# A hybrid encoder step on one Trainium2 core: three plain column tiles, x staged once in two tiles, the first weight pair prepared beside them, operands of the second half built in fixed slots

## The chip, the core and the metric

The kernel runs on one core of a Trainium2 chip. A core has TensorE (PE, matrix products; PEld is its weight load), VectorE (DVE), ScalarE (ACT), GpSimd (POOL) and SyncE (SP, which here issues nearly all DMAs). Each engine works through its own queue in order, and semaphores tie the queues together. The metric is the device time of one execution in microseconds (us).

## The reference, cut to what matters

Two layers on 1024 prompt tokens and 64 sample tokens (1088 columns in all), model width 1024, fp32. Only the first layer, a gated short convolution, is touched by the change:

```
h = rms_norm(x, g)                                  # 1088 x 1024
b, c, xv, z = split(h @ w_in, 4)                    # w_in: 1024 x 4096
u = c * xv
conv = u[t-2]*cw[0] + u[t-1]*cw[1] + u[t]*cw[2]     # causal, per channel
y = (silu(z) * b * conv) @ w_out
x = x + y
```

The second layer is multi-head latent attention over the prompt in chunks of 64 and over a cache of 512 positions for the sample, with a SiLU gate and an output product; a final RMSNorm ends the step. Outputs are both y, the last two convolution rows, and the latents and rope keys.

## The kernel before, in words

Everything is kept transposed: 128 channels on the partitions, tokens on the free axis. To reach fp32 precision each operand is split into a high part in TensorE's reduced fp32 format (a copy on ScalarE) and a low part, the difference (a subtraction on GpSimd or VectorE); a product is then three matmuls: high x high, high x low, low x high.

The input product is worked through in column tiles `ct` of 128 output channels (8 of them) and two token halves of 544 columns (`sc` 0 and 1; `SC` = 544), each half in two chunks of 272 (`NS`).

- **Plain tiles.** For `ct` 0 and 1 the first half is done directly (lines 776 to 834): for each of the four weight parts (order `PARTS`), and for each chunk `c`, `conv_mm` makes 24 matmuls of 272 columns into one PSUM bank, and `conv_evac` takes it out on VectorE. The banks go round in turn (`gps`, line 236), eight of them in this stage. Bank 7 is also where `conv_tail` (line 467) sums the convolution. In tile 0 the order of work on ScalarE, VectorE, GpSimd and TensorE is that of the program text (`keep_order`, `pe_order`); later the Tile framework orders each engine's queue by its own cost model.
- **x.** `x_dma` loads x of the first half in chunks of 272 columns into eight slots of the tile `STG`; chunk 1 goes into the slots of chunk 0. `build_dma` loads the first half a second time, in pieces of 544 columns and four at a time, and then the second half twice: once for the sum of squares (`load_half`, line 592) and once for the operands.
- **Pairs.** All other tiles are done by a seven-product scheme (Strassen's, in Winograd's form) over pairs of weight parts: `u` from parts 1 and 2, `z` from parts 3 and 0. A pair has the seven products p1 to p7, each 4 x 3 matmuls of 272 columns, and PSUM banks 0 to 4 as accumulators; the last two products of a pair (p3, p4) are run inside the next pair. `build(sc, k)` (line 543) makes the token-side operands of the scheme (seven combinations of the four blocks of x, split high and low) for `k` = 0 to 3 into `R2` (first half) or `R1` (second half). `prep` (line 637) makes the weight side: it loads the two parts, splits them as they are (`unit`, 1024 wide, the low part on GpSimd, into three rotating buffer pairs `whi`/`wlo` twice and `bhi`/`blo` once), and makes three sums of 512 columns with PSUM banks 5 and 6 (`S1`, `S2`) and the SBUF tile `t4`; the low parts of the first two are made on VectorE, that of the third (`t4l`) on GpSimd (line 667).
- **Around them.** `run` (line 700) goes through 12 pairs of the first half (`ct` 2 to 7) and 16 of the second, and after each product does one step of `prep` for the next pair and one step of the job list (`side`). The job list holds first the builds of the first half (in tile 1), then `second_half`: loads and squares of the second half, its norm factors, and its builds, which run on GpSimd and ScalarE, with the scaling on ScalarE and VectorE through PSUM. `whole` (line 859) makes pair 12, the first of the second half, wait until the job list is empty.
- **After a product.** `put` in `conv_pairs` (line 743) takes out each of the four blocks of a pair: blocks 11 and 22 are added into the tile `u` or `z`; 12 and 21 are multiplied onto it. For `z` the SiLU of part 3 is applied on ScalarE to blocks 11 and 21 (lines 746 and 751). Block 21 is product p4, in the bank that p1 of the next pair but one takes over.

The rest of the kernel (output product of the convolution, layer 2, final norm) follows behind and is the same text after the change.

Of the kernel before, what the change touches and what calls it, by code (L numbers as in the profile page):

```python
# [19 lines left out]
D = 1024  # L20
# [189 lines left out]
def kernel(ctx, tc, xT, small, w1, w2, w3, w3r, wpair, wqr, wv, wkT, w4,  # L210
# [61 lines left out]
    hi_on = [None]  # L272

    def load_w(src, n, view=None, into=None, lo_engine=None, cuts=None, shared=False):
# [17 lines left out]
        ordered((lo_engine or G).tensor_sub(lo[:, :m], raw[:, :m], r32(hi[:, :m])))  # L292
# [111 lines left out]
    YLB = p1.tile([P, 2, T], F32R, name="YLB")  # L404
# [4 lines left out]
    def yl(k, c0, c1):  # L409
        return YLV[:, k, c0:c1] if k < 6 else YLB[:, k - 6, c0:c1]  # L410

# [6 lines left out]

    def x_dma(c, k):
        XS[k] = STG[:, k * NS:(k + 1) * NS]  # L420
        SP.dma_start(out=XS[k], in_=xT[k][:, c * NS:(c + 1) * NS])
# [116 lines left out]
    def build_dma(sc, k):  # L538
        for i in range(2):
            o = (2 * (k % 2) + i) * SC  # L540
            SP.dma_start(out=STG[:, o:o + SC], in_=xT[k + 4 * i][:, sc * SC:(sc + 1) * SC])

    def build(sc, k):
        h, l = [x[:, :, k] for x in SETS[sc]]
        a, b = [STG[:, (2 * (k % 2) + i) * SC:(2 * (k % 2) + i + 1) * SC] for i in range(2)]
        halves = lambda x: x.rearrange("p (s n) -> p s n", s=2)
# [22 lines left out]
        yield  # L569
        put(1, b)  # L570
# [6 lines left out]
        put(3, a)  # L577
        yield
        put(5, b)
        yield  # L580

    jobs = []

    def side(n=1):

        while n and jobs:
            if next(jobs[0], 0) == 0:
                jobs.pop(0)
            else:
                n -= 1  # L590

    def load_half():

        slot = lambda k: STG[:, (k % 4) * SC:(k % 4 + 1) * SC]
        for k in range(KD):
            if k < 3:
                SP.dma_start(out=slot(k), in_=xT[k][:, SC:])
        yield
        yield
        for k in range(KD):  # L600
            if k + 3 < KD:
                SP.dma_start(out=slot(k + 3), in_=xT[k + 3][:, SC:])
            if k == 0:
                A.activation(out=rb[:, SC:], in_=slot(k), func=AF.Square)
            else:
                A.activation(out=slot(k), in_=slot(k), func=AF.Square)
                G.tensor_add(rb[:, SC:], rb[:, SC:], slot(k))
            yield
# [63 lines left out]
    def product(f, name):  # L672
# [27 lines left out]
    def run(pairs):  # L700

        steps = {}
        for n, f in enumerate(pairs):
            f.set = n % 2
# [1199 lines left out]
```

## Time and profile before

| | |
|---|---|
| time, median of 3 runs | 1140.75 us (1140.28 to 1142.57) |
| profiled execution | 1142.36 us, span 1140.6 us |
| mean granted TensorE clock | 0.971 of full speed |
| PE busy | 1060.4 us (93%), 7099 matmuls |
| PEld busy | 1010.8 us (89%) |
| DVE busy | 769.5 us (67%) |
| ACT busy | 645.8 us (57%) |
| POOL busy | 541.7 us (47%) |
| DMA | 119.02 MB, mean 104 GB/s |
| chain that ended last | PE 58%, DVE 8%, issue 6%, POOL 5%, DMA 4%, ACT 4% |

The page also cuts the span into 40 slices of 28.5 us. In tenths, PE's busy share and its granted clock (9 is 90% or more) are:

```profile
PE   8778997998999999999998999999999999999994
PEclk8897999999999999999998999999999999999997
```

The slices below 9 in the first third lie in the convolution layer, which ends at 427.8 us. Busy times of different engines overlap, and matmuls are pipelined, so that a busy PE is not necessarily at its peak rate; where PE's time goes is read from the count of matmuls in a stage and the time of one.

### The profile page before, as it was taken

Reading aid. Unit: us, or ns where it says so; the run is one execution under the profiler, and the core shown is the slowest. Engines: PE = TensorE matmul, PEld = TensorE weight load, DVE = VectorE, ACT = ScalarE, POOL = GpSimd, SP = SyncE. Lnnn points to the kernel's source line nnn. Section 1 sums busy time; section 2 is a strip of 40 time slices with the busy share of each in tenths; the row PEclk is TensorE's granted clock in tenths of the full one; section 3 lists DMA queues with packets and bytes.
Section 4 is the critical chain, followed back from the end, with each engine's and each line's share of the span. In section 5 each row is a group of like instructions: output and inputs, shape, how many; then the busy total and the mean of one; then the engine's idle time right before and its main releaser. Section 6 shows DMA issues by size and latency. Waiting matters only on the chain.

```text
span 1140.6 us, 19740 instructions
## 1 busy us (share of the span) xinstructions
PE 1060.4 (93%) x7099; PEld 1010.8 (89%) x7099; DVE 769.5 (67%) x1530; ACT 645.8 (57%) x1402; POOL 541.7 (47%) x454
## 2 busy tenths in 40 slices
PE   8778997998999999999998999999999999999994
PEld 7777887898999999999888999899998999988983
DVE  6597665656666655555799533488888888886466
ACT  6246566565656653334542334677877788786452
POOL 3246488777656552112335223254644555464243
PEclk8897999999999999999998999999999999999997
DMA  7226333434232323432313211542243412335224
GB/s 220 88 82 202 103 104 118 128 109 130 81 112 77 109 97 128 147 126 86 100 61 129 76 51 47 144 105 65 61 96 84 101 47 56 75 116 181 89 92 150
DMA packets 60450, 119.02 MB, mean 104 GB/s; under 512 B 8336, under 2 KB 32656, under 8 KB 60352
## 3 DMA queue, kind: packets, MB, share of 16 engines
q1 hardware_dynamic: 60144, 117.43, 34.3%
q8 instruction: 56, 0.92, 0.3%
q14 instruction: 42, 0.34, 0.1%
q10 hardware_dynamic: 144, 0.26, 0.1%
q0 software_dynamic: 64, 0.07, 0.0%
HBM read 83.72 MB, written 16.31 MB: 88 GB/s over the span
## 4 chain that ended last, share of the span: by engine, by line
PE 58%; DVE 8%; issue 6%; POOL 5%; DMA 4%; ACT 4%; SPq 1%; POOLq 0%; ACTq 0%; DVEq 0%
PE PS L299 39%; PE PS L1430 15%; PE PS L1469 4%; DMA QB<-stg 3%; POOL wlo L1708 1%; POOL t4l L622 1%; POOL wlo L622 1%; ACT PH L1482 1%; ACT stg L1546 1%; DVE OL L954 1%; DVE t L666 1%; SPq L1556 1%; DVE PL L1486 0%; DVE qt L1155 0%; DVE SZ L365 0%
## 5 line engine op out<-in xcount | busy, mean ns | idle before, releaser
L299 PE MATMUL PS<-R,whi 128*128 128x272 f32 (+2 forms) x1598 | 368.7, 315 | 30.5 <-DVE z L753 7.7
L299 PEld LDWEIGHTS PS<-R,whi 128*128 128x128 f32 x1598 | 272.0, 192 | 37.6 <-DVE z L753 9.0
L299 PE MATMUL PS<-R,wlo 128*128 128x272 f32 (+2 forms) x856 | 267.5, 314 | 4.8 <-POOL wlo L622 3.6
L299 PEld LDWEIGHTS PS<-R,wlo 128*128 128x128 f32 x856 | 163.6, 192 | 5.7 <-POOL wlo L622 3.8
L292 POOL TENSOR_TENSOR wlo<-wraw,whi 128x1024 fp32r<-128x1024 f32 x32 | 78.8, 2463 | 184.7 <-ACT whi L288 178.8
L1430 PE MATMUL PS<-KB,QB 96*128 96x512 f32 (+11 forms) x576 | 125.4, 355 | 1.3 <-DMA QB<-stg 0.6
L1430 PEld LDWEIGHTS PS<-KB,QB 96*128 96x128 f32 (+1 forms) x576 | 94.4, 190 | 9.9 <-DVE PL L1486 1.1
L1447 DVE TENSOR_REDUCE st<-PS 128x1 f32<-128x1024 f32 (+7 forms) x128 | 94.7, 749 | 11.2 <-PE PS L1430 10.4
L1464 POOL TENSOR_SCALAR Pt<-Pt,st 128x640 f32<-128x640 f32 (+3 forms) x64 | 61.6, 965 | 85.3 <-DVE st L1460 84.7
L1486 DVE TENSOR_TENSOR PL<-PS,PH 128x512 fp32r<-128x512 f32 (+3 forms) x192 | 98.8, 548 | 3.1 <-ACT PH L1482 1.8
L1482 ACT CAST PH<-PS 128x512 fp32r<-128x512 f32 (+3 forms) x192 | 85.4, 496 | 15.4 <-PE PS L1469 14.1
L622 POOL TENSOR_TENSOR wlo<-wraw,whi 128x1024 fp32r<-128x1024 f32 x28 | 67.6, 2414 | 49.5 <-ACT whi L621 49.5
L1430 PE MATMUL PS<-PH,VB 128*128 128x256 f32 x320 | 76.5, 278 | 0.0
L1430 PE MATMUL PS<-PL,VB 128*128 128x256 f32 x320 | 75.2, 281 | 0.2 <-DVE PL L1486 0.2
L299 PE MATMUL PS<-R,bhi 128*128 128x272 f32 x320 | 62.1, 292 | 5.0 <-DVE z L753 2.4
L1456 ACT ACTIVATE Pt<-PS,st 128x640 f32<-128x640 f32 (+3 forms) x64 | 62.1, 970 | 5.7 <-DVE st L1460 2.6
L1430 PEld LDWEIGHTS PS<-PH,VB 128*128 128x128 f32 x320 | 60.7, 190 | 1.4 <-DVE PL L1486 0.8
L1430 PEld LDWEIGHTS PS<-PL,VB 128*128 128x128 f32 x320 | 61.0, 190 | 0.7 <-DVE PL L1486 0.4
L288 ACT CAST whi<-wraw 128x1024 fp32r<-128x1024 f32 (+1 forms) x33 | 34.1, 1032 | 46.2 <-PE PS L299 23.2
L299 PEld LDWEIGHTS PS<-R,bhi 128*128 128x128 f32 x320 | 50.3, 191 | 6.3 <-DVE z L753 3.3
L1469 PE MATMUL PS<-ident,Pt 128*128 128x128 f32 x416 | 55.4, 273 | 0.2 <-ACT Pt L1456 0.2
L1464 POOL TENSOR_SCALAR Ph<-Ph,st 128x512 f32<-128x512 f32 (+3 forms) x64 | 34.2, 535 | 39.0 <-DVE st L1460 28.6
(414 smaller groups left out, 2721.7 us busy)
## 6 DMA issues: line engine op xcount, KB each, us to landing
wraw<-in_w SPq DMA_DIRECT2D x82, 512.0 KB, 3.6
KB<-stg SPq DMA_DIRECT2D x32, 256.0 KB, 3.8
QB<-stg SPq DMA_DIRECT2D x32, 256.0 KB, 4.3
braw<-in_w SPq DMA_DIRECT2D x14, 512.0 KB, 4.6
STG<-in_xT SPq DMA_DIRECT2D x24, 272.0 KB, 3.1
QB<-qr_scratch SPq DMA_DIRECT2D x32, 128.0 KB, 2.9
x<-x_scratch SPq DMA_DIRECT2D x8, 416.0 KB, 3.4
xr<-in_xT SPq DMA_DIRECT2D x16, 192.0 KB, 2.5
```

Source lines behind the costliest of these rows:

```text
L288: ins = A.copy(out=hi[:, :n], in_=raw[:, :n])
L292: ordered((lo_engine or G).tensor_sub(lo[:, :m], raw[:, :m], r32(hi[:, :m])))
L299: ins = PE.matmul(ps, lhsT, rhs, start=start, stop=stop, skip_group_check=more)
L622: eng.tensor_sub(lo, src, r32(hi))
L666: V.tensor_sub(t4, b21, S2)
L1430: pin(PE.matmul(ps, lhsT, rhs, start=start, stop=stop))
L1447: pin(V.tensor_reduce(out=st[:, 0:1], in_=TL["S", h, i], axis=AX.XY, op=ALU.max, negate=True))
L1456: pin(A.activation(out=Pt, in_=TL.pop(("S", h, i)), func=AF.Exp, bias=st[:, 0:1], accum_out=st[:, 1:2]))
L1464: pin(G.tensor_scalar(Pt, Pt, st[:, 2:3], 1.0, op0=ALU.mult, op1=ALU.mult))
L1469: pin(PE.transpose(out=tp[:, j * P:(j + 1) * P], in_=TL["P", h, i][:, (j0 + j) * P:(j0 + j + 1) * P], identity=ident))
L1482: pin(A.copy(out=hi, in_=src))
L1486: pin(V.tensor_sub(lo, src, r32(hi)))
```

## The change

Seven things change in the first layer; `STD` = 3 is the number of plain tiles.

1. Tiles 0, 1 and 2 of the first half are done plainly, and pairs begin at tile 3: 10 pairs in the first half instead of 12.
2. PSUM: tile 0 uses banks 0 to 6 in turn, tiles 1 and 2 use banks 0 to 4; bank 7 is left to `conv_tail`, and 5 and 6 to `S1` and `S2`.
3. x lies in two tiles, `STG` and a new `ST2`, whose place the low parts `YLB` take later (allocated when first needed). All eight slots of 544 columns are there at once (`staged`), so the first half is loaded once. The second half is loaded into a slot when the build of the first half is through with it (`build_first`), once, and serves both the squares (`squares`, through PSUM bank 7, added on VectorE) and the builds.
4. Weights of tiles 1 and 2 are loaded and split one part ahead (`ahead`), and the first pair's `prep` runs beside tile 2, with the rotation shifted so that its first buffers are `bhi`/`blo` and `braw`. In tiles 1 and 2 chunk 0 takes the eight products with the low weight parts last (`lag` = `KD`).
5. In the builds of the first half two of the four splits go from VectorE to GpSimd; in those of the second half the scaling goes to ScalarE and GpSimd, in SBUF.
6. Low parts of the third weight sum (`t4l`) are made on VectorE in the first half, with the sum itself in PSUM; the second half keeps it as it was.
7. The sources of the `z` pair are swapped, so that the SiLU falls on blocks 22 and 12. The second half's work lies in fixed steps of the job list (`at`), and job instructions are ordered behind the last weight split and the last bank copy on their engines (`paced`, `issue_after`).

```diff
...
+    ST2 = p1.tile([P, 2 * T], F32, tag="YL", name="ST2", bufs=1)
+    YLB = []
...
+    def staged(k):
+        o = (2 * (k % 2) + k // 4) * SC
+        return (STG, ST2)[k % 4 // 2][:, o:o + SC]
     def x_dma(c, k):
-        XS[k] = STG[:, k * NS:(k + 1) * NS]
+        XS[k] = staged(k)[:, c * NS:(c + 1) * NS]
         SP.dma_start(out=XS[k], in_=xT[k][:, c * NS:(c + 1) * NS])
...
-    def build_dma(sc, k):
...
     def build(sc, k):
         h, l = [x[:, :, k] for x in SETS[sc]]
-        E = G if sc else V
-        def put(s, x):
+        a, b = staged(k), staged(k + 4)
+        E, F = (G, G) if sc else (V, G)
+        r = rb[:, sc * SC:(sc + 1) * SC]
+        def put(s, x, e):
             o, ol = h[:, s:s + 2], l[:, s:s + 2]
             A.copy(out=o, in_=halves(x))
-            E.tensor_sub(ol, halves(x), r32(o))
-        if sc == 0:
-            build_dma(sc, k)
+            e.tensor_sub(ol, halves(x), r32(o))
         for x, kk in ((a, k), (b, k + 4)):
             g = sm[:, C_NG + kk:C_NG + kk + 1]
             if sc == 0:
-                V.scalar_tensor_tensor(x, x, g, rb[:, :SC], op0=ALU.mult, op1=ALU.mult)
+                V.scalar_tensor_tensor(x, x, g, r, op0=ALU.mult, op1=ALU.mult)
             else:
-                for c in range(2):
-                    t, y = PS[:, 7, :NS], x[:, c * NS:(c + 1) * NS]
-                    A.activation(out=t, in_=y, func=AF.Copy, scale=g)
-                    V.tensor_mul(y, t, rb[:, SC + c * NS:SC + (c + 1) * NS])
-                yield
+                A.activation(out=x, in_=x, func=AF.Copy, scale=g)
+                G.tensor_mul(x, x, r)
         yield
         A.copy(out=h[:, 0], in_=a[:, :NS])
         E.tensor_sub(l[:, 0], a[:, :NS], r32(h[:, 0]))
-        yield
-        put(1, b)
+        put(1, b, F)
         yield
...
-        put(3, a)
-        yield
-        put(5, b)
+        put(3, a, E)
+        put(5, b, F)
+    def build_first(k):
+        yield from build(0, k)
+        yield
+        for kk in (k, k + 4):
+            SP.dma_start(out=staged(kk), in_=xT[kk][:, SC:])
+        yield
+    def squares(k):
+        for kk in (k, k + 4):
+            for c in range(2):
+                q, t = staged(kk)[:, c * NS:(c + 1) * NS], PS[:, 7, :NS]
+                s = rb[:, SC + c * NS:SC + (c + 1) * NS]
+                if kk == 0:
+                    A.activation(out=s, in_=q, func=AF.Square)
+                else:
+                    A.activation(out=t, in_=q, func=AF.Square)
+                    V.tensor_add(s, s, t)
+            yield
...
     def side(n=1):
-        while n and jobs:
+        with ExitStack() as stack:
+            for ins in paced.values():
+                stack.enter_context(tc.issue_after(ins))
+            while n and jobs:
...
-        eng.tensor_sub(lo, src, r32(hi))
+        ins = eng.tensor_sub(lo, src, r32(hi))
+        if eng is G and src.shape[-1] == 1024:
+            paced["lo"] = ins.ins
...
-        pool, tags, bufs = (p1, ("bhi", "blo"), 1) if units[0] % 3 == 0 else (wp[0], ("whi", "wlo"), 2)
+        pool, tags, bufs = (p1, ("bhi", "blo"), 1) if units[0] % 3 == 1 else (wp[0], ("whi", "wlo"), 2)
...
-        pool, tag, bufs = (p1, "braw", 1) if raws[0] % 4 == 0 else (wp[0], "wraw", 3)
+        pool, tag, bufs = (p1, "braw", 1) if raws[0] % 4 == 1 else (wp[0], "wraw", 3)
...
-        t4 = p1.tile([P, 512], F32, tag="t4", name=nm("t4"), bufs=1)
-        V.tensor_sub(t4, b21, S2)
-        give(parts_of(*own(4), t4, G), "p4")
+        if f.sc:
+            t4 = p1.tile([P, 512], F32, tag="t4", name=nm("t4"), bufs=1)
+            V.tensor_sub(t4, b21, S2)
+            give(parts_of(*own(4), t4, G), "p4")
+        else:
+            V.tensor_sub(S2, b21, S2)
+            give(parts_of(*own(4), S2, V), "p4")
...
-            A.copy(out=t, in_=ps)
+            paced["copy"] = A.copy(out=t, in_=ps).ins
...
-                if silu and block == 11:
+                if silu and block == 22:
                     A.activation(out=o, in_=o, func=AF.Silu)
...
-            if silu and block == 21:
+            if silu and block == 12:
                 A.activation(out=ps, in_=ps, func=AF.Silu)
...
-        fz = Pair((w1[ct][3], w1[ct][0]), sc, put_z)
+        fz = Pair((w1[ct][0], w1[ct][3]), sc, put_z)
...
-    for ct in range(2):
+    STD = 3
+    pairs = [f for sc, cts in ((0, range(STD, KD)), (1, range(KD))) for ct in cts for f in conv_pairs(ct, sc)]
+    split_psum(g=(0, 7))
+    ahead = []
+    for ct in range(STD):
...
-                                 [R2[:, REG - n:REG - n + 1024] for n in (2048, 1024)])
+                                 [R1[:, REG - n:REG - n + 1024] for n in (2048, 1024)])
...
-            jobs.extend(build(0, k) for k in range(4))
+            split_psum(g=(0, 5))
+            turns["g"][1] = 2
+            jobs.extend([build_first(0), build_first(1), squares(0), build_first(2), squares(1), build_first(3)])
         else:
-            for part in PARTS:
-                W = load_w(w1[ct][part], 1024)
+            for pi, part in enumerate(PARTS):
+                W = ahead.pop() if ahead else load_w(w1[ct][part], 1024)
+                if pi < 3 or ct + 1 < STD:
+                    ahead.append(load_w(w1[ct + (pi == 3)][PARTS[(pi + 1) % 4]], 1024))
+                    paced["lo"] = lo_on[0]
                 for c in range(2):
-                    conv_evac(ct, u, z, part, c, conv_mm(c, W))
+                    conv_evac(ct, u, z, part, c, conv_mm(c, W, (KD, 0)[c]))
                     side(2)
+                if ct == STD - 1:
+                    with tc.issue_after(lo_on[0]), tc.issue_after(hi_on[0]):
+                        step(0, (0, 1, 1, 4)[pi])
...
     def second_half():
-        yield from load_half()
...
+        todo = {}
+        def at(t, f):
+            todo.setdefault(t, []).append(f)
+        def factors():
+            todo[8] = [rstd([rb[:, SC:]], rb[:, SC:], D, SC)]
+        at(3, factors)
         for k in range(4):
-            yield from build(1, k)
-            yield
-            if k < 2:
-                build_dma(1, k + 2)
-    jobs.append(second_half())
+            steps = build(1, k)
+            for t in (0, 5, 6, 13):
+                at(10 + 13 * k + t, lambda steps=steps: next(steps, None))
+        for t in range(64):
+            for f in todo.get(t, []):
+                f()
+            yield
+    jobs.extend([squares(2), squares(3), second_half()])
+    step(1)
-    pairs[12].whole = True
-    run(pairs)
+    pairs[2 * (KD - STD)].whole = True
+    run()
...
```

## Rows read from the trace of the kernel before

**Rows 1.** Windows: length, busy (x count) of PE, PEld, DVE, ACT, POOL; PEclk; DMA.

```profile
0.00:53.00 53.00, 40.01 (x241) 38.11 (x242) 30.77 (x76) 24.02 (x49) 16.55 (x16) 0.84 0.52 166
53.00:78.40 25.40, 24.21 (x193) 24.00 (x192) 22.86 (x42) 11.30 (x22) 8.90 (x5) 1.00 0.28 92
78.40:102.80 24.40, 13.72 (x63) 11.71 (x63) 20.75 (x30) 13.07 (x24) 12.64 (x8) 0.65 0.43 127
102.80:216.00 113.20, 99.58 (x739) 97.20 (x738) 70.33 (x152) 68.18 (x134) 86.98 (x62) 0.95 0.40 126
216.00:281.00 65.00, 59.74 (x462) 57.99 (x460) 39.56 (x80) 38.59 (x78) 46.50 (x27) 1.00 0.35 111
281.00:427.80 146.80, 141.84 (x1117) 140.51 (x1118) 92.50 (x194) 86.73 (x188) 87.78 (x53) 1.00 0.31 98
```

**Rows 2.** Timeline of PE: start, length, instruction; first matmuls of two neighbouring products.

```profile
102.77 0.41 PE L299 MATMUL PS<-R,bhi 128*128 128x272 f32 x2
...
104.27 0.41 PE L299 MATMUL PS<-R,t1h 128*128 128x272 f32 x2
```

**Rows 3.** Timeline of PE in tile 0, at the longest wait (idle before, and releaser).

```profile
38.91 0.82 PE L299 MATMUL PS<-R,whi 128*128 128x272 f32 x2 [6.09 <-DVE y L484]
```

**Rows 4.** Timeline of DVE in tile 0, from 31 to 50 us.

```profile
31.73 0.44 DVE L514 TENSOR_TENSOR u<-PS,rb2kp 128x272 f32<-128x272 f32 x1
...
38.41 0.44 DVE L484 TENSOR_TENSOR y<-PS,z 128x272 f32<-128x272 f32 x1
44.60 0.16 DVE L321 TENSOR_SCALAR rsv<-PS 128x3 f32<-128x3 f32 x1 [5.75 <-PE PS L299]
...
45.21 2.29 DVE L329 TENSOR_TENSOR rst<-rsy 128x3 f32<-128x3 f32 x1
...
48.90 0.16 DVE L331 SCALAR_TENSOR_TENSOR rsy<-rst,rsy 128x3 f32<-128x3 f32 x1
```

**Rows 5.** Waits of PE, 78.4 to 102.8 us: total, times, longest.

```profile
PE PS L299 <- POOL wlo L622: 3.6, 1, 3.6
PE PS L299 <- DVE t1l L622: 3.6, 1, 3.6
```

**Rows 6.** Timeline of DVE and POOL from 59 to 65 us.

```profile
59.02 0.72 DVE L552 TENSOR_TENSOR R<-STG,R 128x544 fp32r<-128x544 f32 x1
...
60.81 3.21 POOL L292 TENSOR_TENSOR wlo<-wraw,whi 128x1024 fp32r<-128x1024 f32 x1 [5.81 <-ACT whi L288]
...
62.13 2.47 DVE L552 TENSOR_TENSOR R<-STG,R 128x544 fp32r<-128x544 f32 x1 [0.36 <-ACT R L551]
```

**Rows 7.** Waits of DVE, 102.8 to 281 us, the longest.

```profile
DVE t L666 <- POOL t4l L622: 21.8, 14, 5.2
```

**Rows 8.** Waits of PE, 102.8 to 281 us, the longest.

```profile
PE PS L299 <- DVE z L753: 6.2, 5, 1.9
```

**Rows 9.** Waits of PE, 281 to 428 us, the longest.

```profile
PE PS L299 <- DVE z L753: 5.5, 6, 1.6
```

**Rows 10.** Groups of POOL instructions, 103 to 281 us: busy us, mean ns; idle before.

```profile
L622 POOL TENSOR_TENSOR wlo<-wraw,whi 128x1024 fp32r<-128x1024 f32 x14 | 33.6, 2398 | 18.4 <-ACT whi L621 18.4
L622 POOL TENSOR_TENSOR t4l<-t,t4h 128x512 fp32r<-128x512 f32 x14 | 18.0, 1289 | 7.1 <-ACT t4h L621 6.8 <-DMA STG<-in_xT 0.2
...
L552 POOL TENSOR_TENSOR R<-STG,R 128x544 fp32r<-128x544 f32 x12 | 16.2, 1360 | 3.0 <-ACT R L551 3.0
...
L572 POOL TENSOR_TENSOR STG<-STG 128x272 f32<-128x272 f32 x4 | 3.1, 776 | 0.3
```

**Rows 11.** Timeline of all engines from 299.8 to 302.95 us.

```profile
299.89 0.39 ACT L752 ACTIVATE PS<-PS 128x272 f32<-128x272 f32 x1
...
300.70 1.05 ACT L621 CAST bhi<-braw 128x1024 fp32r<-128x1024 f32 x1 [0.42 <-PE PS L299]
...
301.81 0.69 DVE L666 TENSOR_TENSOR t<-wraw,PS 128x512 f32<-128x512 f32 x1 [1.21 <-POOL t4l L622]
...
302.41 0.43 DVE L753 TENSOR_TENSOR z<-PS,z 128x272 f32<-128x272 f32 x1
```

More of the change, by code (lines that the diff above doesn't have):

```diff
@@ L271 @@
     WN = [1024, 2]
-    hi_on = [None]
+    hi_on, lo_on = [None], [None]
     def load_w(src, n, view=None, into=None, lo_engine=None, cuts=None, shared=False):
@@ L291, in load_w @@
         m = n // 2 if shared else n
-        ordered((lo_engine or G).tensor_sub(lo[:, :m], raw[:, :m], r32(hi[:, :m])))
+        ins = (lo_engine or G).tensor_sub(lo[:, :m], raw[:, :m], r32(hi[:, :m]))
+        lo_on[0] = ins.ins
+        ordered(ins)
         if shared:
@@ L403 @@
     YLV = R2[:, KD * T:].rearrange("p (k t) -> p k t", t=T)
-    YLB = p1.tile([P, 2, T], F32R, name="YLB")
+    ST2 = p1.tile([P, 2 * T], F32, tag="YL", name="ST2", bufs=1)
+    YLB = []
     def yh(k, c0, c1):
@@ L409, in yl @@
     def yl(k, c0, c1):
-        return YLV[:, k, c0:c1] if k < 6 else YLB[:, k - 6, c0:c1]
+        if k < 6:
+            return YLV[:, k, c0:c1]
+        if not YLB:
+            YLB.append(p1.tile([P, 2, T], F32R, tag="YL", name="YLB", bufs=1))
+        return YLB[0][:, k - 6, c0:c1]
     nconv = p1.tile([P, KD, 4], F32, name="nconv")
@@ L536, with halves @@
     POS = dict(p1=0, p2=1, p4=2, p6=3, p7=4, p3=5, p5=6)
-    def build_dma(sc, k):
-        for i in range(2):
-            o = (2 * (k % 2) + i) * SC
-            SP.dma_start(out=STG[:, o:o + SC], in_=xT[k + 4 * i][:, sc * SC:(sc + 1) * SC])
+    def halves(x):
+        return x.rearrange("p (s n) -> p s n", s=2)
     def build(sc, k):
         h, l = [x[:, :, k] for x in SETS[sc]]
-        a, b = [STG[:, (2 * (k % 2) + i) * SC:(2 * (k % 2) + i + 1) * SC] for i in range(2)]
-        halves = lambda x: x.rearrange("p (s n) -> p s n", s=2)
-        E = G if sc else V
-        def put(s, x):
+        a, b = staged(k), staged(k + 4)
+        E, F = (G, G) if sc else (V, G)
+        r = rb[:, sc * SC:(sc + 1) * SC]
+        def put(s, x, e):
             o, ol = h[:, s:s + 2], l[:, s:s + 2]
             A.copy(out=o, in_=halves(x))
-            E.tensor_sub(ol, halves(x), r32(o))
-        if sc == 0:
-            build_dma(sc, k)
+            e.tensor_sub(ol, halves(x), r32(o))
         for x, kk in ((a, k), (b, k + 4)):
@@ L576, in build @@
         yield
-        put(3, a)
+        put(3, a, E)
+        put(5, b, F)
+    def build_first(k):
+        yield from build(0, k)
         yield
-        put(5, b)
+        for kk in (k, k + 4):
+            SP.dma_start(out=staged(kk), in_=xT[kk][:, SC:])
         yield
+    def squares(k):
[9 more added lines that the diff above has]
+            yield
     jobs = []
+    paced = {}
     def side(n=1):
-        while n and jobs:
[L587 to L597, printed above, removed]
-        yield
-        yield
[L600 to L608, printed above, removed]
+        with ExitStack() as stack:
+            for ins in paced.values():
+                stack.enter_context(tc.issue_after(ins))
+            while n and jobs:
+                if next(jobs[0], 0) == 0:
+                    jobs.pop(0)
+                else:
+                    n -= 1
     class Pair:
@@ L698, in product, with step, run @@
             f.put(12, 0, ps, f.p6)
[L700 to L704, printed above, removed]
-        def step(n, k=1):
-            for _ in range(k):
-                if n < len(pairs):
-                    if n not in steps:
-                        steps[n] = prep(pairs[n])
-                    next(steps[n], None)
-        step(0, 6)
-        step(1, 1)
+    steps = {}
+    def step(n, k=1):
+        for _ in range(k):
+            if n < len(pairs):
+                if n not in steps:
+                    pairs[n].set = n % 2
+                    steps[n] = prep(pairs[n])
+                next(steps[n], None)
+    def run():
         for n, f in enumerate(pairs):
@@ L841, in second_half @@
     def second_half():
-        yield from load_half()
-        yield from range(1, 5)
-        build_dma(1, 0)
-        build_dma(1, 1)
-        end = rstd([rb[:, SC:]], rb[:, SC:], D, SC)
-        yield from range(1, 12)
-        end()
-        yield from range(1, 3)
-        for k in range(4):
-            yield from build(1, k)
-            yield
-            if k < 2:
-                build_dma(1, k + 2)
-    jobs.append(second_half())
-    pairs = [f for sc, cts in ((0, range(2, KD)), (1, range(KD))) for ct in cts for f in conv_pairs(ct, sc)]
-    pairs[12].whole = True
-    run(pairs)
+        todo = {}
[4 more added lines that the diff above has]
+        at(3, factors)
+        for k in range(4):
+            steps = build(1, k)
[4 more added lines that the diff above has]
+                f()
+            yield
+    jobs.extend([squares(2), squares(3), second_half()])
+    step(1)
+    pairs[2 * (KD - STD)].whole = True
+    run()
     SP.dma_start(out=o_conv, in_=nconv.rearrange("p a b -> p (a b)"))
```

1 line of the change is left out of this document (added).

## The prediction

> **What bounds the kernel now.** I read the busy time by stage first [rows 1]. TensorE (PE) is the engine everything waits for. Its own rate comes from one product at full clock: the first matmuls of two neighbouring products start at 102.77 and 104.27 us, 12 matmuls of 272 columns apart [rows 2], so 0.1254 us each. A plain column tile (2 token chunks x 4 weight parts x 8 k x 3 = 192 matmuls) is then worth 24.1 us; a weight pair (7 products x 4 k x 3 = 84) 10.54 us, a tile done by pairs 21.1 us. Against these prices each stage of [rows 1] shows what is lost:
>
> - 53.0 to 78.4 (second plain tile): 193 matmuls are 24.2 us, lost 1.2.
> - 78.4 to 102.8 (change to pairs): 63 matmuls are 7.9 us, lost 16.5, and the mean clock is 0.65.
> - 102.8 to 216 (second half's operands are built): 739 matmuls, 20 of them the small ones of the norm (about 3 us); 719 x 0.1254 + 3 = 93.2, lost 20.0 at clock 0.95.
> - 216 to 281: 462 are 57.9, lost 7.1.
> - 281 to 427.8, where the convolution ends: 1117 are 140.0, lost 6.8 at full clock.
>
> So 52 us are lost between 53 and 428, plus a stall of 6.09 us in the first tile [rows 3]. Behind 428 nothing is edited; I carry it over unchanged.
>
> **The change part by part**
>
> *First tile.* PE stands 6.09 us before the second product of chunk 1 [rows 3], because the bank it wants is bank 7, where the convolution of chunk 0 is still being summed until VectorE's (DVE's) multiply of 38.41 is done [rows 4]. With seven banks in the rotation that product gets bank 0, free since the evacuation of 31.73 [rows 4]. PE then runs on from about 32.9 and is done with this product at 35.9. The next bound is DVE's order, which is written out here: the norm chain of chunk 1 started at 44.60, after a wait for PE, and ended with the step of 48.90 [rows 4], 4.4 us, 2.1 of them one step that took 2.29 us beside a GpSimd (POOL) weight split. In the new order it can start when the multiply of 38.41 ends, at 38.9, and ends between 41.2 (no collision) and 43.3, against 49.06. Gain 5.7 to 7.9; I take **-7.0**. x's second chunk no longer waits for its slot; I count nothing for that, since the written order of DVE's work ahead of 31.73 stays.
>
> *One more plain tile.* 24.1 - 21.1 = **+3.0**, on PE, certain.
>
> *Change to pairs.* Of the 16.5 us lost, the two largest waits are for the first pair's own parts, 3.6 us each [rows 5]; the operands of the first half were late too. Now the pair's weights are prepared beside the third tile in buffers of their own (bhi/blo), and x lies staged, so that no build waits for a load. Steps: 16 calls of two job steps in two tiles, 24 steps needed, so the last is issued half a tile early. What remains is whether POOL and DVE keep up. POOL in the two tiles: 8 weight splits x 2.40 (eight loads less two made earlier, and the pair's two), 8 operand splits of 544 moved from DVE x 1.36, five 272-wide products x 0.78 [rows 10] = 34.0. DVE operations that read two SBUF tensors: per k three of 544 at 0.72 [rows 6] and five of 272 at 0.44 [rows 4], four k: 17.4. The trace shows that these exclude POOL: the same split takes 0.72 at 59.02 and 2.47 at 62.13, where it ends just after the POOL split of 60.81, which itself took 3.21 instead of 2.40 [rows 6, 10]. The two sums make 51.4 against 48.2 us of PE work, and the last weight split (2.4) isn't needed before the seventh product. The excess is about 1; at nine tenths of perfect packing (my estimate) about 6. I leave 5 us of the 16.5, clock included: **-11.5** (bounds: all gone, -16.5; nothing gone, 0). Inside the two tiles the loss rises from 1.2 to 2.2: **+1.0** (bounds -1.2, +5).
>
> The Trainium skill ("SBUF — State Buffer", "SBUF: two separate sides") calls this pair of ports an exclusive lock between GpSimd and a DVE operation with two SBUF inputs, held for a whole instruction. By that rule alone the two sums add, and moving splits from DVE to POOL lengthens the total (1.36 for 0.72); the trace agrees (2.47 against 0.72).
>
> *Pairs of the first half.* In the dense stage DVE waits 21.8 us in 14 waits for POOL's t4l [rows 7]: the next t4 needs the one buffer, POOL's queue is full of builds, and behind that subtraction DVE's evacuations stand, for which PE waits (z multiplies alone 6.2 us [rows 8]). The edit takes the t4 split from POOL to DVE and t4 into PSUM, so this chain is gone in the first half; it costs DVE 0.7 us per pair, hidden (DVE is busy 70 of 113 us [rows 1]). POOL per operand k now: two multiplies and three splits of 544 at 1.36, one split and four sums of 272 at 0.78 [rows 10] = 10.7 us, every 13 calls; in 13 calls (13/7 pairs) come 3.7 weight splits of 2.40 = 8.9. Together 19.6 us where PE needs 13/7 x 10.54 = 19.6. POOL is exactly full, without t4l. Before, eight steps of a build and 8/7 pairs with t4l asked 8.0 + 5.5 + 1.5 = 15.0 in 12.0 us. A weight part can start when the part two pairs back is through (third product, 4.5 us into the pair) and needs a copy of 1.05 [rows 11], the split of 2.4 and some waits before the next pair: 2 us of slack; the builds are ordered behind the splits. I take 0.4 us lost per pair, 4 for 10 pairs.
>
> *Swapped gate sources.* In the second half PE waits 5.5 us, six times, for a z multiply [rows 9], at the start of every other pair. DVE's queue shows it: the t4 subtraction of 301.81 waits 1.21 for POOL's t4l, and the z multiply that frees PE's bank stands behind it; its SiLU on ScalarE came at 299.89 [rows 11]. The u pairs, which have no SiLU on that block, give no such wait in this stage. After the swap the block that frees the bank has no SiLU and can stand ahead of the subtraction. The SiLU moves to a bank that is wanted five products (7.5 us) later. I take 3 us lost in 16 pairs.
>
> The 26 pairs so lose 7 where 33.9 (20.0 + 7.1 + 6.8) are lost now: **-26.9** (bounds: all gone -33.9; in the first half still the dense rate, 20.0 us in 93.2/10.54 = 8.8 pairs, 2.3 each, and in the second 6.8 in 13.3 pairs, 0.5 each: 23 + 8 = 31, that is -3).
>
> *The rest:* second x pass (16 loads less in issue, none on the path), squares from POOL to DVE (14 additions of 0.44 from PSUM, 6 of them in the tiles; there DVE has the 17.4 above, some 16 of evacuations and 5 of weight preparation, so 41 of 48 us, which covers them; up to +3 if not, within the +5 above).
>
> Sum: -7.0 + 3.0 - 11.5 + 1.0 - 26.9 = **-41.4**. The profiled execution took 1142.36 us (span 1140.6), 1.6 above the median of 1140.75; from the median 1099.4, I say **1100**.
>
> **The rivals**
>
> 1. *POOL is over-full in the first half.* For it: 19.6 of 19.6 us leaves nothing for the gaps between instructions, and a build comes in lumps of 5.3 us. Against: the waits of now run through t4l, which leaves POOL. The 10 pairs then lose 23 instead of 4: 1100 + 19 = 1119. Chance 0.20.
> 2. *The port decides the tiles.* 51.4 us with blocked time on DVE on top: builds and evacuations lag, the loss at the change to pairs stays at 16.5 and the tiles lose 2 more: 1100 + 11.5 + 2 = 1113. For it: one split blocked for 1.75 us with POOL busy 21.5 of 49.8 us [rows 1]; after, about 34 of 48. It is the Trainium skill's lock ("SBUF — State Buffer") taken at its word. Against: x no longer arrives late, and weights are split one part ahead. Chance 0.16.
> 3. *Slower.* POOL's queue is in order. If the build lump stands ahead of both weight parts of the next pair, PE waits the whole lump, 5.3 us, and loses another 1.9 to the clock (the 0.65 of the change to pairs [rows 1]): 7.2 in each of 7 pairs is 50, against which the gain of 41 is gone: 1150. It decides from 41/7 = 5.9 us lost per lump. Against: the builds are tied behind the last weight split, and 2 us of slack come first. Chance 0.05.
> 4. *The first tile's stall only moves* (DVE's chain and its collision eat it): 1107, faster all the same. Chance 0.05.
>
> **How the numbers follow.** The forecast has 0.54. At its best every bound is met: -7.9 + 3.0 - 16.5 - 1.2 - 33.9 = -56.5, 1084. Rivals 1 and 2 lie at 1119 and 1113, both at once at 1132. The range 1086 to 1121 leaves out the extremes and the slower case. All but the slower case and a sliver are faster by more than 0.2% (2.3 us, what a measurement can tell): faster 0.94, same 0.01, slower 0.05.
>
> **What would show it.** Right: no 6 us gap near 38; the first pair's products follow the third tile's at full clock, at about 95 to 100; DVE has no wait for t4l before the second half begins; z multiplies release PE hardly ever; the convolution ends near 387. Wrong: clock under 0.9 between 90 and 110 (rival 2); PE waiting for POOL weight splits with POOL busy above nine tenths (rivals 1, 3).

## The result and the profile after

The changed kernel takes 1113.38 us (median of 4 runs, 1110.66 to 1115.04) against 1141.07 for the kernel before, timed beside it: a ratio of 0.9753, 95% interval 0.973 to 0.9777. So 27.7 us went, where 41 were forecast. The profiled execution took 1114.31 us, span 1112.5, mean granted clock 0.980. Matmuls are 7123 (24 more), PE is busy 1056.6 us, DVE 749.8, ACT 637.5, POOL 539.7, and the DMAs moved 114.55 MB (4.5 less: one read of x).

The windows by stage, with boundaries at the changed kernel's own stages (columns as in [rows 1]): tile 0; tiles 1 and 2; the first two pairs; the builds of the second half; the change of halves; the second half; the rest of the kernel.

```profile
0.00:45.80 45.80, 38.00 (x240) 36.29 (x240) 29.24 (x77) 24.43 (x51) 16.61 (x17) 0.89 0.51 168
45.80:97.40 51.60, 49.46 (x385) 48.37 (x386) 35.19 (x70) 23.88 (x44) 33.13 (x20) 1.00 0.38 113
97.40:131.00 33.60, 26.91 (x173) 26.07 (x173) 21.40 (x53) 15.91 (x32) 11.52 (x6) 0.85 0.22 74
131.00:203.00 72.00, 70.94 (x563) 70.46 (x562) 46.99 (x95) 47.85 (x92) 62.47 (x44) 1.00 0.37 129
203.00:272.00 69.00, 64.22 (x486) 62.50 (x486) 45.40 (x92) 44.89 (x92) 53.59 (x34) 0.98 0.34 115
272.00:398.10 126.10, 124.57 (x989) 124.12 (x989) 79.58 (x171) 77.32 (x169) 82.05 (x48) 1.00 0.30 97
398.10:1112.50 714.40, 682.48 (x4297) 642.34 (x4295) 491.96 (x963) 403.23 (x911) 280.30 (x286) 0.98 0.34 97
```

Priced as in the prediction (0.1254 us per matmul, 3 us for the 20 small ones), the stages lose 3.3, 11.4, 1.4, 8.0 and 2.1 us. The dense stage, which lost 20.0 us [rows 1], is nearly at PE's pace, with GpSimd busy 62.47 of 72 us. The largest loss now stands in the first two pairs (of the 173 matmuls from 97.4 to 131, 20 are the small ones of the second half's norm), where the clock is 0.85. The convolution ends at 398.1 instead of 427.8. The untouched rest took 714.4 instead of 712.8.

Tile 0 went as forecast. The two rows of PE and DVE that answer to [rows 3, 4]: the 6.09 us gap is gone, the norm chain starts at 38.84 and ends at 41.38, and PE's wait before the chain's result is 1.93 us.

```profile
41.43 0.93 PE L301 MATMUL PS<-ident,rsy 128*128 128x128 f32 x6 [1.93 <-DVE rsy L333]
```

```profile
38.84 0.15 DVE L323 TENSOR_SCALAR rsv<-PS 128x3 f32<-128x3 f32 x1
...
41.22 0.16 DVE L333 SCALAR_TENSOR_TENSOR rsy<-rst,rsy 128x3 f32<-128x3 f32 x1
```

What costs the 11.4 us can be read in two chains. First PE's waits from 97.4 to 131 (total, times, longest), which answer to [rows 5], then the timeline of DVE, ACT and PE around the longest of them. `acc` of line 602 is the sum of squares, `p` a product copied out of its bank.

```profile
PE PS L301 <- ACT p L702: 3.9, 2, 2.8
PE PS L301 <- DVE acc L602: 1.6, 1, 1.6
PE PS L301 <- ACT acc L346: 1.1, 1, 1.1
```

```profile
104.64 0.44 DVE L496 TENSOR_TENSOR y<-PS,z 128x272 f32<-128x272 f32 x1 [2.45 <-DMA y_scratch<-y]
105.12 0.40 ACT L601 ACTIVATE PS<-ST 128x272 f32<-128x272 f32 x1 [3.57 <-DVE u L540]
...
107.26 0.38 ACT L702 COPY p<-PS 128x272 f32<-128x272 f32 x1
107.69 0.58 PE L301 MATMUL PS<-R,whi 128*128 128x272 f32 x2 [2.82 <-ACT p L702]
```

The first chain: DVE's last multiply of tile 2 (L496) waits 2.45 us until the DMA has carried off y of chunk 0, since y has one buffer. Its input is the convolution sum in bank 7. The squares of the second half's x, which stand in the first pair's job steps, go through bank 7 too, so the first of them (L601) waits 3.57 us at the head of ScalarE's queue. (The profile names the 0.06 us memset of L540, which follows the multiply in DVE's queue and ends within 0.02 us of it.) The copy of a product out of PE's bank (L702) stands behind them, and PE waits 2.82 us for it.

Behind that wait the clock fell. The next groups of three matmuls start 0.68 us apart until about 111.4, against 3 x 0.1254 = 0.38; the granted clock of that stretch is 0.54.

```profile
108.08 0.43 PE L301 MATMUL PS<-R,wlo 128*128 128x272 f32 x1
...
108.76 0.43 PE L301 MATMUL PS<-R,wlo 128*128 128x272 f32 x1
...
111.45 0.29 PE L301 MATMUL PS<-R,wlo 128*128 128x272 f32 x1
```

The second chain comes from the squares directly: the second half's norm begins with ten small matmuls on their sum, and PE waits 1.65 us until DVE has added the last square. Behind this wait the clock fell again, and for longer, from 115.7 to 121.3 (granted 0.50, the lower of its two levels, 1.2 GHz).

```profile
114.13 1.68 PE L301 MATMUL PS<-ones,acc 128*128 128x1 f32 x10 [1.65 <-DVE acc L602]
...
116.50 0.66 PE L301 MATMUL PS<-R,t1h 128*128 128x272 f32 x2
...
121.82 0.41 PE L301 MATMUL PS<-R,t2h 128*128 128x272 f32 x2
```

The third wait listed (L346) is for the norm factors' copy out of a bank; it stays in experiment 3. The waits listed are 6.6 us. At the lower clock 17 matmuls took 3.7 us and 24 took 5.6, 1.6 and 2.6 us more than at full clock. Together that is 10.8 of the 11.4 us.

In the dense stage DVE's waits for t4l, 21.8 us in 14 [rows 7], are gone; from 97.4 to 272 there are 4.6 us in 4, all for pairs of the second half. From 272 to 398.1 PE waits once, 1.0 us, for a z multiply, where it waited 5.5 us in six [rows 9].

### The profile page after: what moved, and what is told of

It is laid out like the page before. It is cut to its first block, busy times and chain, and to the rows that moved or that the text cites. A ratio compares the mean times of both kernels' runs of the same rounds, so it can differ in the third digit from the quotient of the medians.

```text
span 1112.5 us, 19655 instructions
## 1 busy us (share of the span) xinstructions
PE 1056.6 (95%) x7123; PEld 1010.2 (91%) x7123; DVE 749.8 (67%) x1516; ACT 637.5 (57%) x1388; POOL 539.7 (49%) x453
## 2 busy tenths in 40 slices
DMA packets 58145, 114.55 MB, mean 103 GB/s; under 512 B 8080, under 2 KB 32400, under 8 KB 58048
## 4 chain that ended last, share of the span: by engine, by line
PE 66%; DVE 5%; issue 5%; POOL 4%; DMA 3%; ACT 3%; SPq 0%; POOLq 0%; ACTq 0%; DVEq 0%
PE PS L301 44%; PE PS L1459 17%; PE PS L1498 5%; DMA QB<-stg 2%; POOL wlo L1737 1%; DVE OL L983 1%; ACT PH L1511 1%; ACT stg L1575 1%; POOL t4l L632 0%; DMA wraw<-in_w 0%; POOL wlo L632 0%; SPq L1585 0%; DVE PL L1515 0%; DMA wraw<-in_wpair 0%; PE PS L1305 0%
## 5 line engine op out<-in xcount | busy, mean ns | idle before, releaser
L301 PEld LDWEIGHTS PS<-R,whi 128*128 128x128 f32 x1662 | 276.7, 191 | 21.5 <-ACT p L702 5.6
L292 POOL TENSOR_TENSOR wlo<-wraw,whi 128x1024 fp32r<-128x1024 f32 x36 | 88.5, 2460 | 170.7 <-ACT whi L288 158.0
L632 POOL TENSOR_TENSOR wlo<-wraw,whi 128x1024 fp32r<-128x1024 f32 x26 | 62.4, 2401 | 26.7 <-ACT whi L631 24.0
L288 ACT CAST whi<-wraw 128x1024 fp32r<-128x1024 f32 (+1 forms) x37 | 38.2, 1032 | 38.0 <-PE PS L301 20.4
```

Of the source, the lines that this page charges most:

```text
L288: ins = A.copy(out=hi[:, :n], in_=raw[:, :n])
L292: ins = (lo_engine or G).tensor_sub(lo[:, :m], raw[:, :m], r32(hi[:, :m]))
L301: ins = PE.matmul(ps, lhsT, rhs, start=start, stop=stop, skip_group_check=more)
L632: ins = eng.tensor_sub(lo, src, r32(hi))
```

## The experiments

Twelve kernels, each timed beside the kernel before. Ratios are to that kernel, with their 95% intervals. The kernel before took 1140.88 to 1142.21 us beside them, so a difference of 1 us between two changed kernels means nothing. The windows keep the changed kernel's boundaries; a kernel that runs ahead has later work in them.

**1. The banks of tile 0 alone**, in the kernel before:

```diff
+    split_psum(g=(0, 7))
     for ct in range(2):
...
             keep_order[0] = False
+            split_psum(g=(0, 8))
```

> The kernel before with one edit: tile 0 takes banks 0 to 6 in turn instead of 0 to 7. Theory (the first tile's stall is the bank alone): the 6.09 us wait goes, the second norm chain ends near 41.2 as in the changed kernel, and 7 us come off: 1134. Rival (staging x once is what brings the first tile forward): the wait stays near 6 us or only moves, 1138 to 1141. Rival (later stages give it back, since the builds that are late at the change to pairs do not get earlier): tile 0 ends 7 us earlier and the loss between 78 and 103 grows by as much, about 1140.

Measured: 1134.36 us, ratio 0.9946 (0.9927 to 0.9965). PE's waits in tile 0 and behind it:

```profile
40.34 0.94 PE L299 MATMUL PS<-ident,rsy 128*128 128x128 f32 x6 [1.84 <-DVE rsy L331]
75.96 0.82 PE L299 MATMUL PS<-R,whi 128*128 128x272 f32 x2 [10.19 <-DVE y L484]
```

The bank alone brings tile 0 forward. The stage behind it is no better: PE waits 10.19 us at 75.96, for the same multiply (L484), as tile 1 still goes through all eight banks. But it doesn't eat the gain. The first theory holds.

**2. A buffer of its own for y of chunk 1**, in the changed kernel:

```diff
-        y = p1.tile([P, NS], F32, tag="cv", name=nm("y"), bufs=1)
+        if sc == 0 and c == 1:
+            y = p1.tile([P, 512], F32, tag="t4", name=nm("y"), bufs=1)[:, :NS]
+        else:
+            y = p1.tile([P, NS], F32, tag="cv", name=nm("y"), bufs=1)
```

> The changed kernel, with a buffer of its own for the convolution's result y of chunk 1 in the first half. Theory (the 11.4 us lost from 97 to 131 start with y: its one buffer is held by a DMA, so bank 7 is held, so the squares stand at the head of ScalarE's queue and the copies of p behind them): VectorE's wait of 2.45 us for the DMA goes, PE's wait of 2.8 us at 107 shrinks below 1, the clock there stays up, 3 to 6 us come off: 1107 to 1110. Rival (the squares themselves fill ScalarE and VectorE in these slots, whatever y does): at most 1 us, 1112 to 1114.

Measured: 1109.7 us, ratio 0.9720 (0.9703 to 0.9738). PE's longest wait in the same stretch, then the one that was 2.82 us:

```profile
PE PS L301 <- DVE acc L605: 3.2, 1, 3.2
```

```profile
105.31 0.52 PE L301 MATMUL PS<-R,whi 128*128 128x272 f32 x2 [0.41 <-ACT p L705]
```

DVE's wait for the DMA is gone and the wait for the copy of p before this product fell from 2.82 to 0.41 us, as the theory has it; the loss of the stretch went from 11.4 to 8.5. But PE's wait for the square sums grew from 1.6 to 3.2: the squares have a price of their own. The interval reaches just into the changed kernel's (0.973 to 0.9777), so the size of this gain is rough.

**3. The squares in the third tile**, in the changed kernel:

```diff
-            jobs.extend([build_first(0), ..., squares(1), build_first(3)])
+            jobs.extend([build_first(0), ..., squares(1), build_first(3), squares(2), squares(3)])
...
-    jobs.extend([squares(2), squares(3), second_half()])
+    jobs.extend([iter(range(1, 5)), second_half()])
```

> The changed kernel, with the squares of the last two operand pairs put into the spare job steps of the third plain tile, and four empty steps where they stood. Theory (the squares in the first pair's slots cost it): PE's waits for the copy of p and for the square sums go (2.8 and 1.65 us, and the clock behind them), the loss from 97 to 131 falls from 11.4 to 3 or 4: 1105 to 1107. Rival (the third tile has no room: its loads for these squares have only just been issued, and they stand in the queues ahead of the evacuations): the loss moves into the tile, 1111 to 1118.

Measured: 1106.19 us, ratio 0.9696 (0.9681 to 0.9710). The tiles and the first pairs:

```profile
45.80:97.40 51.60, 48.79 (x379) 47.45 (x378) 36.00 (x74) 25.67 (x49) 32.07 (x20) 1.00 0.38 113
97.40:131.00 33.60, 30.35 (x242) 29.93 (x241) 23.00 (x54) 18.38 (x35) 15.31 (x9) 1.00 0.32 108
```

242 matmuls in the stretch instead of 173, at full clock: 222 x 0.1254 + 3 = 30.8 of 33.6 us, lost 2.8 instead of 11.4. PE has no wait for the square sums. The tiles have room for the squares (379 matmuls against 385).

**4. Two plain tiles instead of three** (`STD = 2`), in the changed kernel.

> The changed kernel with two plain tiles instead of three. PE has 3.0 us less to do. Theory (the third tile is the cover under which the operands and the first pair's weights get ready): the work of 24 job steps stands against 16 calls' worth of steps in one tile, and the change to pairs loses some 15 to 20 us again instead of 11: 1115 to 1122. Rival (the staged x alone makes the builds early, the third tile is only cost): 1110 to 1112.

Measured: 1118.33 us, ratio 0.9804 (0.9790 to 0.9819). Behind the second tile:

```profile
71.20:97.40 26.20, 11.93 (x63) 11.11 (x62) 21.56 (x39) 12.20 (x25) 12.31 (x8) 0.61 0.32 99
```

```profile
80.17 0.79 PE L301 MATMUL PS<-R,t1h 128*128 128x272 f32 x2 [6.82 <-DVE z L534]
89.18 0.60 PE L301 MATMUL PS<-R,t1h 128*128 128x272 f32 x1 [6.63 <-ACT R L562]
```

By the same price 18.3 of these 26.2 us are lost. The kernel is 5 us slower with 3.0 us less work for PE: the third tile is worth some 8 us of cover.

**5. The gate's sources in their old order**, in the changed kernel:

```diff
-                if silu and block == 22:
+                if silu and block == 11:
...
-            if silu and block == 12:
+            if silu and block == 21:
...
-        fz = Pair((w1[ct][0], w1[ct][3]), sc, put_z)
+        fz = Pair((w1[ct][3], w1[ct][0]), sc, put_z)
```

> The changed kernel with the sources of the z pair in their old order (SiLU on blocks 11 and 21). Theory (the SiLU on the block that frees PE's bank made the waits at the start of every other pair): in the second half PE's waits for a z multiply come back, 0.6 to 1.6 us in every other pair, some 5 us in all, and as much again in the first half: 1117 to 1121. Rival (those waits came from the t4 subtraction ahead of it in VectorE's queue, whichever block has the SiLU): within 1 us of 1113.

Measured: 1122.7 us, ratio 0.9836 (0.9796 to 0.9875), so the swap is worth some 9 us, a little more than the theory's band. The size is rough, as the four runs lie between 1119.97 and 1129.77. PE's waits for the z multiply from 217 to the end of the convolution, then from 131 to 217:

```profile
PE PS L301 <- DVE z L766: 5.4, 6, 1.5
```

```profile
PE PS L301 <- DVE z L766: 3.8, 3, 2.4
```

The six waits for a z multiply are back in their old size. From 131 to 217, where the changed kernel has none of them, there are three, though the third sum is off GpSimd in these pairs; the SiLU is enough for them.

**6. The third weight sum on GpSimd again in the first half** (`if True:` for `if f.sc:` in `prep`), in the changed kernel.

> The changed kernel with the third weight sum's low part on GpSimd again in the first half, and the sum in its SBUF tile t4. Theory (VectorE's waits for t4l lost the 20 us of the dense stage): GpSimd is asked for 2.4 us more per 13 calls than the 19.6 that PE's pace leaves, VectorE waits for t4l again, and the stage from 131 to 203, which loses 1.4 us now, loses 8 to 15: 1120 to 1128. Rival (it is the even spread of the builds over fixed steps that ended the loss, and the third sum's place matters little): 1113 to 1116.

Measured: 1126.8 us, ratio 0.9863 (0.9824 to 0.9901). The dense stage, and DVE's longest wait for GpSimd from 131 to 217:

```profile
131.00:203.00 72.00, 64.79 (x502) 63.14 (x501) 41.04 (x86) 44.63 (x86) 62.52 (x46) 1.00 0.33 103
```

```profile
DVE t L679 <- POOL t4l L632: 13.4, 6, 4.2
```

502 matmuls in 72 us are 63.0, lost 9.0 instead of 1.4. GpSimd is as busy as in the changed kernel (62.52 against 62.47 us), with fewer matmuls served (502 against 563). Fixed steps alone don't empty the queue; t4l must leave GpSimd.

**7. All splits of the first half's builds on VectorE** (`(V, V)` for `(V, G)`), in the changed kernel.

> The changed kernel with all four splits of the first half's builds on VectorE, as before. GpSimd has 10.9 us less in the two tiles, VectorE 5.8 more. Theory (VectorE's own queue is what is full in the tiles): the evacuations and builds come later, the tiles lose 3 to 6 us more: 1116 to 1120. Rival (the port that the two engines share decides, and each split costs it less on VectorE, 0.72 against 1.36): equal or faster, 1110 to 1113.

Measured: 1108.67 us, ratio 0.9701 (0.9675 to 0.9727): below the changed kernel's 0.9753 (0.973 to 0.9777). So this part of the change cost about 5 us: the theory is refuted, and the rival has the direction. The tiles and the first pairs of this kernel, then the longest wait of DVE in the tiles of the changed kernel:

```profile
45.80:97.40 51.60, 48.93 (x383) 47.81 (x382) 46.30 (x83) 24.96 (x47) 24.65 (x13) 1.00 0.39 122
97.40:131.00 33.60, 29.14 (x218) 28.51 (x217) 20.25 (x51) 18.62 (x37) 10.52 (x5) 0.95 0.25 90
```

```profile
DVE ST L577 <- POOL R L563: 10.4, 2, 6.4
```

PE does the same work in the tiles (383 against 385), though DVE is busier by 11 us; the gain lies in the first pairs (218 against 173), where PE's waits for the copy of p fall from 3.9 to 0.2 us; the one for the square sums grows from 1.6 to 3.2. In the changed kernel DVE stood 10.4 us because the next sum overwrites the block that GpSimd's split is still to read; its evacuations came late by that, and tile 2's last multiply with them (it starts at 104.64; here at 100.44, behind a wait of 2.14 for the same DMA). How much of the 5 us is this wait and how much the shared port (the prediction's second rival), this run doesn't tell apart.

**8. Without the tied order** (no `issue_after` in `side`), in the changed kernel.

> The changed kernel without the orders that tie job instructions behind the last weight split and the last bank copy. Theory (GpSimd is full in the dense stage, so a build ahead of a weight split makes PE wait): PE waits for weight splits or bank copies appear between 131 and 203, 5 to 15 us in all: 1118 to 1128. Rival (the fixed steps already keep the queues in a good order): 1111 to 1115.

Measured: 1136.18 us, ratio 0.9938 (0.9917 to 0.9959). The dense stage and PE's longest waits from 131 to 217:

```profile
131.00:203.00 72.00, 54.95 (x349) 52.47 (x348) 30.98 (x64) 33.30 (x63) 58.45 (x48) 0.79 0.24 82
```

```profile
PE PS L301 <- ACT p L700: 10.3, 4, 4.4
```

349 matmuls are 43.8 us, so 28.2 of 72 are lost, more than in the kernel before. Without the ties nearly the whole gain is gone: 23 us, 8 more than the theory's band. Where PE waits is mostly not the weight split (GpSimd, 3.5 us in two waits) but the bank copy, and it stands in ScalarE's queue: a build's copy (L562) waits there for GpSimd, with the copy of p behind it.

```profile
165.71 0.64 ACT L562 CAST R<-ST 128x544 fp32r<-128x544 f32 x1 [5.42 <-POOL ST L579]
166.26 0.38 ACT L700 COPY p<-PS 128x272 f32<-128x272 f32 x1
166.69 0.82 PE L301 MATMUL PS<-R,t2h 128*128 128x272 f32 x2 [2.37 <-ACT p L700]
```

The run takes off both ties at once, that behind the weight split and that behind the bank copy; what each is worth stays open.

**9. Experiments 2 and 3 together.**

> The squares in the third tile and y's own buffer, both. Theory (y's buffer hurts only through the squares behind it): with the squares gone from the first pair it is worth nothing more, 1105 to 1107, within 1 us of the squares alone (1106). Rival (two separate costs): the 3 us of y's buffer come on top, 1102 to 1104.

Measured: 1107.13 us, ratio 0.9694 (0.9667 to 0.9721), no different from experiment 3. With about 3 us to either side the interval alone would still allow the rival's 3 us; the trace speaks for the theory, as the one wait for the copy of p left from 97.4 to 131 is 1.9 us here and 2.1 in experiment 3. With the squares gone, y's buffer has no price that these runs show.

**10. Experiments 3 and 7 together.**

> The squares in the third tile and all splits of the first half's builds on VectorE. Theory (in the tiles VectorE stood 10.4 us waiting for GpSimd's splits, so moving them back costs it little and lets the builds end early): the two gains of 7 and 5 us overlap, since both empty the first pair's slots; PE has no wait for squares, 1103 to 1106. Rival (VectorE is then over-full, 46 of 51.6 us and 3.5 more): the evacuations come late and the tile loses it again, 1107 to 1112.

Measured: 1104.2 us, ratio 0.9673 (0.9650 to 0.9695). The first pairs hold 254 matmuls, 32.3 of 33.6 us. Its interval overlaps with that of experiment 3, so that the second gain on top isn't proved; they overlap, as expected.

**11. Experiment 10, with the third weight sum on VectorE and in PSUM in both halves** (`if False:` for `if f.sc:`).

> The kernel with squares in the tile and all splits on VectorE, and in the second half too the third weight sum on VectorE and in PSUM. Theory (the waits left at the start of the second half, 4.3 us between 217 and 272, come from t4l in GpSimd's queue behind the reload of y): PE's waits for u and z multiplies after 217 go, 3 to 5 us less than without it: 1099 to 1103. Rival (the extra 0.7 us per pair on VectorE delays the evacuations as much): within 1 us of it.

Measured: 1096.92 us (1095.25 to 1097.04), ratio 0.9603 (0.9587 to 0.9618): the fastest of all. The change of halves:

```profile
203.00:272.00 69.00, 69.00 (x551) 69.00 (x551) 51.17 (x103) 48.79 (x102) 49.02 (x29) 1.00 0.38 128
```

PE has no wait there at all, and one of 1.0 us from 272 on. The convolution ends at 381.97 against 388.52 in experiment 10; 7.3 us are more than the 3 to 5 expected. In the traces 1.6 us of the lead is there at 203 already (1420 matmuls against 1407), ahead of the edited sums; from 203 to 272 come 4.4 more (551 against 516).

**12. Experiment 7 with the same edit**, the squares left where they are.

> The changed kernel with all splits and all third weight sums on VectorE, the squares left where they are. If the second half's gain is its own, it comes in the same size here: 3 to 5 us under the 1109 of the splits alone, 1104 to 1106. If it is not, 1108 to 1110.

Measured: 1105.39 us, ratio 0.9673 (0.9651 to 0.9695), inside the expected band, but the interval overlaps with experiment 7's (0.9675 to 0.9727). In this kernel the gain is not proved by itself; in experiment 11 it is.

## Why the prediction was right, and where it was off

Sign and range held: faster, 1113.4 in a range of 1086 to 1121. The range also took in the prediction's first two rivals (1119 and 1113), so that it held says little by itself; the mechanisms are carried by experiments 1, 5, 6 and 8. The sum was 13 us too large. Its price per matmul stands (the start times shown give 0.1250, from 94.34 to 97.35 in the changed kernel 24 matmuls give 0.1254). Term by term, on the profiled executions:

| step | forecast | measured |
|---|---|---|
| first tile | -7.0 | -7.2 (ends at 45.8, not 53.0) |
| one more plain tile | +3.0 | +3.0 (24 matmuls more, priced) |
| loss inside the tiles | +1.0 | +2.1 (1.2 to 3.3) |
| change to pairs | -11.5 | -5.1 (16.5 to 11.4) |
| all later pairs | -26.9 | -22.4 (33.9 to 11.5) |
| rest of the kernel | 0 | +1.6 |
| sum | -41.4 | -28.0 |

- **First tile.** Right in place, size and cause; experiment 1 takes it alone.
- **Change to pairs: the step that failed.** The prediction saw the change as weights and operands that must be ready, and they were: the first pair's p1 starts at 97.35 right behind the third tile, and its first two products ran at full clock. The waits for the pair's own parts (3.6 us each before) are gone; the 11.4 are another loss, in waits for bank copies and square sums. Under "the rest" it priced the squares' move to VectorE at nothing, "which covers them; up to +3 if not", and looked at the additions in the tiles alone; the eight squares in the first pair's slots were not looked at as what they are, work through bank 7 with ScalarE's queue behind it. What stands in the queue behind them was not asked. They measure some 7 us (experiment 3, and experiment 2 for the part that goes through y and bank 7).
- **The builds' moved splits.** The prediction counted GpSimd and DVE sums for the port and found them just full (rival 2 at 1113). GpSimd's sum was right (34.0 us forecast, 33.13 measured). The total came out as that rival says, but by another way, so this agreement is chance: the tiles lost 2 us more, the first pair's parts came in time, the rival's sign (a clock under 0.9 between 90 and 110) did not come, with 0.95 there, and the trace names a data wait, DVE for GpSimd's split, 10.4 us. The port is seen as well: in the changed kernel's timeline below two scalings of 544 columns (0.78 each where GpSimd does nothing) take 4.49 together, while GpSimd runs a split of 1.37 and one of 2.89. The Trainium skill ("GPSIMD Engine Reference", "4.1 Engine selection") sends an elementwise operation on a tile to VectorE and calls GpSimd about twice as slow for two inputs. The rows agree, 0.72 against 1.36 us [rows 6, 10]. Experiment 7, with these splits back on VectorE, is 5 us faster, though it doesn't show that the shorter split is why.

```profile
53.55 1.37 POOL L563 TENSOR_TENSOR R<-STG,R 128x544 fp32r<-128x544 f32 x1 [5.05 <-ACT R L562]
53.86 4.49 DVE L568 SCALAR_TENSOR_TENSOR ST<-ST,sm,acc 128x544 f32<-128x544 f32 x2
54.88 2.89 POOL L292 TENSOR_TENSOR wlo<-wraw,whi 128x1024 fp32r<-128x1024 f32 x1
```

- **Dense stage.** t4l as a cause is shown by experiment 6 (9.0 us lost from 131 to 203, where the changed kernel loses 1.4); 4 us lost were forecast for ten pairs, 1.4 measured from 131 to 203, which holds 6.7 of them. GpSimd, counted as exactly full, was busy 0.87 of this stage, and PE waited for none of its splits there. The prediction named the ties in half a sentence against rival 3; experiment 8 shows that they carry 23 us. Rival 3 saw the kind of fault, a build ahead in an in-order queue and PE standing, but put it in GpSimd's queue; the larger part appeared in ScalarE's (10.3 us for bank copies against 3.5 for weight splits).
- **Gate swap.** Right, and larger than thought: some 9 us. The prediction put the t4 subtraction beside the SiLU as a cause; in the first half the SiLU was enough (experiment 5).
- **Change of halves.** 8.0 us lost from 203 to 272, where the forecast counted 3 for the whole second half. Of these, 3.5 are lost by 217: PE waits 1.80 us at 205.91 for a copy of p behind the last build's copies on ScalarE, and the clock falls behind it. Most of the rest comes where the third sum, kept on GpSimd in the second half, waits behind the reload of y (L511 below); DVE's next sum waits for it, and PE for the multiply behind that. This was not foreseen, and experiment 11 removes it; its wait for the copy of p (1.8 us) is still there, ahead of 203.

```profile
252.84 1.37 POOL L511 TENSOR_TENSOR YLB<-STG,R 128x544 fp32r<-128x544 f32 x1
254.16 1.29 POOL L632 TENSOR_TENSOR t4l<-t,t4h 128x512 fp32r<-128x512 f32 x1
255.49 0.69 DVE L679 TENSOR_TENSOR t<-wraw,PS 128x512 f32<-128x512 f32 x1 [2.25 <-POOL t4l L632]
258.21 0.52 PE L301 MATMUL PS<-R,whi 128*128 128x272 f32 x2 [1.66 <-DVE u L758]
```

The difference of 1.6 us in the rest is within the spread of single executions and was not studied.

## What to carry to other kernels

Price a moved instruction by the resource it borrows, not by its engine's busy share: here eight squares of 0.4 us cost some 7 us, because they shared a bank with the convolution's sum, stood ahead of the bank copies in an in-order queue, and were themselves waited for by the norm. Spare steps beside plain work (the third tile) are the place for such work, not the first steps after a change of scheme. Where an engine is nearly full, its load is not all that decides whether TensorE waits: the same work without the ordering cost 23 us (experiment 8), and yet one more split per pair on the full engine cost 13 (experiment 6).

## What the runs showed of the hardware that was not expected

A wait of the same length was followed by a lower clock in one run and not in another. PE's wait of 1.80 us at 205.91 in the changed kernel and its wait of 1.81 at 197.59 in experiment 3 come before the same product of a pair, each behind 7 us or more without a wait. Behind the first, groups of three matmuls come to start 0.68 us apart (208.81 and 209.49), and the mean clock from 203 to 217 is 0.88. Behind the second they stay at 0.38 (198.45 and 198.83), and the clock from 195 to 209 is 1.00. So a stall of this size can't be priced by its length alone.

```profile
205.91 0.52 PE L301 MATMUL PS<-R,whi 128*128 128x272 f32 x2 [1.80 <-ACT p L702]
...
208.81 0.65 PE L301 MATMUL PS<-R,bhi 128*128 128x272 f32 x2
```

```profile
197.59 0.52 PE L301 MATMUL PS<-R,whi 128*128 128x272 f32 x2 [1.81 <-ACT p L702]
...
198.83 0.41 PE L301 MATMUL PS<-R,whi 128*128 128x272 f32 x2
```
